# Feed-forward weights loaded and split two chunks at a time, in slabs of eight raw and six split places

## The chip, the cores and the metric

The kernel runs on one core of a Trainium2 chip. The metric is device time in microseconds of one execution, lower is better; the runs before have a median of 2163.3 us.

## The reference

A two-layer encoder on 256 tokens of width 2048, all in float32. Layer 0 mixes tokens by pooling and grouped-query attention, layer 1 by a bidirectional mLSTM. After each mixer comes the same feed-forward layer, which the change is about:

```python
def conv_ffn(x, w_up, conv_w, conv_b, w_down):
    u = x @ w_up                                   # 2048 -> 2 * 5632
    ...
    u = c[0] * up[:, :-2] + c[1] * up[:, 1:-1] + c[2] * up[:, 2:] + conv_b.astype(u.dtype)
    gate, val = jnp.split(u, 2, axis=-1)
    return (jax.nn.silu(gate) * val) @ w_down      # 5632 -> 2048
...
x = x + mixed
x = x + conv_ffn(rms_norm(x, norm_ffn[layer]), w_up[layer], conv_w[layer], conv_b[layer], w_down[layer])
```

## The kernel before

**Weights.** All weights come as one stream of 890 chunks in the order of use, each 128 partitions x 1024 columns (512 KB, rows of 4 KB). `Stream` handles them. `load` starts a DMA on SP's queue into a raw tile w. `split` makes of w a high half, rounded to float32r by a cast on ScalarE (ACT, L152), and a low half, what is left, by a subtraction on VectorE (DVE, L153); both go into a split tile hl. TensorE (PE) multiplies high by high, high by low and low by high. `next` hands out the next chunk's hl and calls `ahead`, which keeps `la` chunks loaded and `sa` chunks split ahead of the one in use. Outside the feed-forward layers there are six raw and four split tiles; inside them one more of each (`more`, L1145), so seven and five, taken in turn.

**The feed-forward layer.** A list from `_ffn_plan` sets TensorE's order by hand. "n" steps are the up-projection (tiles named up, four chunks for 256 of the output columns), "d" steps the down-projection (dn), both of ordinary chunks. "s" steps belong to units (tiles p1 to p6, named by layer, chunk of the hidden width and half: p1_0_21 is layer 0, chunk 2, half 1), which compute four column blocks of the up-projection with seven products instead of eight, out of sums of weight blocks and of activations (sx, made by DVE at the layer's start in `sums`). There are five units a layer; a unit has 28 chunks: 16 for the first half, 12 for the second, where two of three are added in place on DVE before their split (kind "left", L140). Sums of the first half are mostly made ahead by accumulating DMAs from HBM to HBM (tiles G, started by `make_step` when a certain chunk is loaded, on SP and POOL). `UNITS` says between which slots of the list a unit's chunks are strewn. An up or down chunk is 16 or 12 matmuls on TensorE, a unit's chunk 6.

**Who sets the order.** TensorE's order is written by hand; that of ACT, DVE and SP is set by a scheduler when the program is built, and each engine then works its list strictly in order. `Weave` lets small tasks (transposes, convolution tails) run between matmul groups by a planned time.

## Time and profile before

| | |
|---|---|
| runs | 2163.64, 2163.3, 2160.51 us; median 2163.3 |
| profiled execution | span 2160.9 us, granted clock 1.000; no own time beside the span is given, and the fastest run is within 0.4 us of it |
| stages, from the span's start | attention to 256 us, first feed-forward layer to 968, mLSTM to 1448, second feed-forward layer to 2157 |
| SP's loads of 512 KB | about 6 us from issue to landing |
| DMA share of the 16 engines | 0.98 to 0.99 in the first feed-forward layer, 0.74 to 0.91 in the second |

In the rows shown below a group's line reads: source line, engine, operation, output<-inputs by the program's names without numbers, shape and count, then busy time in all and mean nanoseconds of one, then the idle time of that engine just before and what ended it. A timeline row is start, length, engine, line, operation and count, with the idle time before it in brackets. L numbers are lines of this kernel.

### The profile page before, as it was taken

The page shows a single profiled execution, that of the slowest core. Times are in us where ns is not written, and L with a number is a line of the kernel's source. Part 1 is how long each engine was busy: PE and PEld are TensorE (multiplying, and loading weights), DVE is VectorE, ACT ScalarE, POOL GpSimd, SP SyncE. Part 2 cuts the span into 40 slices and gives each one's busy share as a digit, 9 for nine tenths or more (in the row PEclk, how much of TensorE's full clock was granted, in tenths as well). Part 3 has the DMA queues.
Part 4 walks back from the last instruction along what each step waited for, and adds up shares of the span by engine and source line. Part 5 has one row for each costly group of instructions (what it writes and reads, how often), then busy time and mean ns, then how long its engine had stood idle before and what let it go on. Part 6 is the DMA issues. An engine that isn't in the chain of part 4 may idle for free.

```text
span 2160.9 us, 31049 instructions
## 1 busy us (share of the span) xinstructions
PE 2153.2 (100%) x10896; PEld 1826.7 (85%) x10896; DVE 1717.8 (79%) x2400; ACT 1309.2 (61%) x1840; POOL 276.0 (13%) x344
## 2 busy tenths in 40 slices
PE   9999999999999999999999999999999999999999
PEld 7888888888888888888888888888888888888887
DVE  7686698989889797866777677669898888879785
ACT  7665566766557576655454544556676666757663
POOL 0122111111111111111111111110000010000000
PEclk9999999999999999999999999999999999999999
DMA  8878899999999999979998998887999999877773
GB/s 325 257 229 246 256 262 345 316 332 320 308 325 308 351 332 339 319 200 250 250 263 251 256 253 244 258 244 223 312 286 306 302 297 288 272 249 238 259 245 119
DMA packets 204702, 596.15 MB, mean 276 GB/s; under 512 B 26010, under 2 KB 28354, under 8 KB 204546
## 3 DMA queue, kind: packets, MB, share of 16 engines
q1 hardware_dynamic: 167776, 531.43, 70.1%
q0 software_dynamic: 33696, 59.00, 18.3%
q10 hardware_dynamic: 3074, 3.75, 0.9%
q8 instruction: 85, 1.39, 0.2%
q14 instruction: 71, 0.58, 0.1%
HBM read 591.93 MB, written 119.58 MB: 329 GB/s over the span
## 4 chain that ended last, share of the span: by engine, by line
PE 93%; DMA 5%; DVE 1%; ACT 0%; issue 0%; SPq 0%; ACTq 0%; DVEq 0%
PE up L268 23%; PE dn L268 20%; PE p L268 16%; PE op L268 8%; PE mo L268 4%; PE mk L268 4%; PE mq L268 4%; PE mv L268 3%; PE qproj L268 3%; PE kproj L268 1%; PE vproj L268 1%; PE tr L1081 1%; DMA w<-G 1%; PE pool L268 1%; DMA w<-in_m_in 1%; DMA w<-in_up 1%
## 5 line engine op out<-in xcount | busy, mean ns | idle before, releaser
L153 DVE TENSOR_TENSOR hl<-w,hl 128x1024 fp32r<-128x1024 f32 (+2 forms) x892 | 1075.6, 1218 | 319.9 <-ACT hl L152 302.0
L152 ACT CAST hl<-w 128x1024 fp32r<-128x1024 f32 (+2 forms) x891 | 924.8, 1048 | 646.9 <-PE up L268 98.9
L268 PE MATMUL up<-xx,hl 128*128 128x512 f32 (+1 forms) x3072 | 560.2, 337 | 0.0
L268 PEld LDWEIGHTS up<-xx,hl 128*128 128x128 f32 x3072 | 486.7, 188 | 76.7
L268 PE MATMUL dn<-hl,g 128*128 128x512 f32 x2064 | 491.8, 391 | 0.0
L268 PEld LDWEIGHTS dn<-hl,g 128*128 128x128 f32 x2064 | 385.1, 188 | 79.0
L268 PE MATMUL p<-hl,sx 128*128 128x512 f32 x960 | 250.6, 390 | 0.0
L124 POOL DMA_DIRECT2D G<-in_q x160 | 132.0, 830 | 875.5 <-DMA G<-in_q 872.4
L268 PEld LDWEIGHTS p<-hl,sx 128*128 128x128 f32 x960 | 176.0, 188 | 34.4 <-DVE hl L153 0.6
L128 POOL DMA_DIRECT2D G<-G x144 | 127.9, 888 | 538.2 <-DMA G<-in_q 243.0
L268 PE MATMUL p<-hl,xx 128*128 128x512 f32 x720 | 193.5, 390 | 0.0
L268 PEld LDWEIGHTS p<-hl,xx 128*128 128x128 f32 x720 | 130.8, 188 | 24.0
L268 PE MATMUL mk<-xx,hl 128*128 128x512 f32 (+1 forms) x512 | 92.5, 338 | 1.4 <-DVE hl L153 1.4
L268 PE MATMUL mq<-xx,hl 128*128 128x512 f32 (+1 forms) x512 | 92.2, 337 | 0.0
L268 PE MATMUL mv<-hl,xx 128*128 128x512 f32 (+2 forms) x480 | 91.8, 350 | 0.0
L268 PE MATMUL op<-hl,cat 128*128 128x512 f32 x384 | 91.6, 393 | 0.0
L268 PE MATMUL mo<-hl,xx 128*128 128x512 f32 x384 | 90.5, 391 | 0.0
L268 PEld LDWEIGHTS mk<-xx,hl 128*128 128x128 f32 x512 | 79.0, 188 | 13.1 <-DVE hl L153 1.8
L268 PE MATMUL op<-hl,mcat 128*128 128x512 f32 x384 | 89.5, 392 | 0.0
L268 PEld LDWEIGHTS mq<-xx,hl 128*128 128x128 f32 x512 | 79.3, 188 | 11.6
L268 PEld LDWEIGHTS mv<-hl,xx 128*128 128x128 f32 x480 | 78.3, 189 | 11.2
L268 PEld LDWEIGHTS op<-hl,mcat 128*128 128x128 f32 x384 | 71.5, 188 | 14.6
(242 smaller groups left out, 1865.2 us busy)
## 6 DMA issues: line engine op xcount, KB each, us to landing
w<-in_up SPq DMA_DIRECT2D x192, 512.0 KB, 6.1
w<-in_dn SPq DMA_DIRECT2D x176, 512.0 KB, 6.2
w<-in_m_in SPq DMA_DIRECT2D x124, 512.0 KB, 6.0
w<-in_q SPq DMA_DIRECT2D x88, 512.0 KB, 6.2
G<-in_q SPq DMA_DIRECT2D x144, 256.0 KB, 6.4
G<-G POOLq DMA_DIRECT2D x144, 256.0 KB, 7.5
w<-G SPq DMA_DIRECT2D x72, 512.0 KB, 6.1
w<-in_a_in SPq DMA_DIRECT2D x46, 512.0 KB, 6.1
```

Of the source, the lines that this page charges most:

```text
L124: pin(add.dma_start(G[r, 0:512], src[r, 512:1024], accum_op=ALU.add))
L128: pin(add.dma_start(G[:, at : at + 512], G[:, of : of + 512], accum_op=ALU.add))
L152: (self.nc.vector.tensor_copy if i + c == 0 else self.nc.scalar.copy)(hl[:, 0, c : c + n], w[:, c : c + n])
L153: self.nc.vector.tensor_sub(hl[:, 1, c : c + n], w[:, c : c + n], hl[:, 0, c : c + n].bitcast(F32))
L268: pe.matmul(out_, lhsT, rhs, start=start, stop=stop, skip_group_check=True)
L1081: pe.transpose(tr[:, j, t * P : t * P + P], src[:, c : c + P], ident)
```

## The change

In the feed-forward layers chunks are loaded and split in pairs. The raw tiles become places of one slab of six, and of a second slab of two inside these layers; the split tiles places of a slab of four and one of two. A pair takes two neighbouring places. An up or down pair comes with one DMA of 1 MB (rows of 8 KB, the host lays them out so); a unit's chunks still come with DMAs of their own. One cast and one subtraction of 2048 columns split a pair. Three pairs of split places and four of raw ones are in use. The list of steps is counted in pairs, so the units' chunks are strewn in pairs too (`UNITS` halved), and a step of TensorE yields every two chunks. Two sums of kind "left" in one pair become one instruction. Which place is taken is chosen by `Slots.free`; outside these layers chunks stay single.

```diff
+class Slots:
+    def free(self, pair, extra):
+        n = [(100 * b, t.shape[1]) for b, t in enumerate(self.parts) if b == 0 or extra]
+        every = [o + k for o, m in n for k in range(0, m, 2 if pair else 1)]
+        free = [j for j in every if not self.busy.get(j) and not (pair and self.busy.get(j + 1))]
+        return min(free, default=None, key=lambda j: (
+            not pair and not self.busy.get(j ^ 1), max(self.age.get(j, -1), self.age.get(j + pair, -1)), j))
...
 class Stream:
+        self.raw = Slots(wpool.tile([P, 6, CH * P], F32, tag="w", name="w"))
+        self.hls = Slots(spool.tile([P, 4, 2, CH * P], F32R, tag="hl", name="hl"))
...
     def load(self, pieces=1):
-        w = self.home(i, True).tile([P, CH * P], F32, tag="w", name=f"w{i}")
+        pair = self.pair(i)
+        j = self.raw.free(pair, self.extra(i))
+        if j is None:
+            return False
...
+        if pair and got[0][0] == got[1][0] == "half" and got[0][1] is got[1][1] and got[0][2] == 0:
+            sync.dma_start(self.raw.both(j), got[0][1].rearrange("p (a n) -> p a n", a=2))
...
     def split(self, then=None):
+        if pair:
+            w, hl = self.raw.both(self.w[i][0]), self.hls.both(j)
+            self.nc.scalar.copy(hl[:, :, 0], w)
+            self.nc.vector.tensor_sub(hl[:, :, 1], w, hl[:, :, 0].bitcast(F32))
...
     def next(self):
+        if i:
+            self.hls.give(self.hl.pop(i - 1))
...
-                    if q < KT // 4 - 1:
+                    if q == 1:
                         yield
...
-            st.la, st.sa, st.more = 7, 3, (lp(f"fw{layer}", 1), lp(f"fh{layer}", 1), st.at + len(_ffn_plan(layer)))
+            st.raw.parts[1:] = [lp(f"fw{layer}", 1).tile([P, 2, CH * P], F32, tag="w", name=f"fw{layer}")]
+            st.hls.parts[1:] = [lp(f"fh{layer}", 1).tile([P, 2, 2, CH * P], F32R, tag="hl", name=f"fh{layer}")]
+            n = (st.n_load - st.at) % 2
+            st.la, st.sa, st.wide = 9, 4, (st.n_load + n, st.at + 2 * len(_ffn_plan(layer)))
...
-    ((1, 1, 17, 38, 2), (2, 1, 45, 64, 2), (3, 1, 71, 100, 3), (4, 1, 107, 129, 2), (5, 1, 136, 158, 2)),
+    ((1, 1, 8.5, 19, 2), (2, 1, 22.5, 32, 2), (3, 1, 35.5, 50, 3), (4, 1, 53.5, 64.5, 2), (5, 1, 68, 79, 2)),
```

The rows below are lists of the built programs, engine by engine; "x3" are three in a row. In the old program a tile's name has the chunk's number (hl199 is chunk 199's split tile); in the new one w_90 and hl_91 are the slabs of six and four places, fw0 and fh0 those of two, in layer 0.

First place: the second half of layer 0's unit 2 (p1, p5, p6 with 0_21), beside up chunk up0_15. ACT before:

```order
L152 CAST hl193_4776<-w193_4705 128x1024
L152 CAST hl195_4798<-w195_4736 128x1024
L152 CAST hl196_4825<-w196_4752 128x1024
L152 CAST hl199_4869<-w199_4796 128x1024
L152 CAST hl197_4837<-w197_4774 128x1024
L152 CAST hl198_4848<-w198_4785 128x1024
L152 CAST hl200_4880<-w200_4818 128x1024
```

DVE before:

```order
L153 TENSOR_TENSOR hl196_4825<-w196_4752,hl196_4825 128x1024
L140 TENSOR_TENSOR w197_4774<-w197_4774 128x512
L153 TENSOR_TENSOR hl199_4869<-w199_4796,hl199_4869 128x1024
L153 TENSOR_TENSOR hl197_4837<-w197_4774,hl197_4837 128x1024
L153 TENSOR_TENSOR hl198_4848<-w198_4785,hl198_4848 128x1024
L153 TENSOR_TENSOR hl200_4880<-w200_4818,hl200_4880 128x1024
```

Chunk 199 stands ahead of 197 and 198 on both engines. With five places its cast needs chunk 194's, which TensorE must have left. TensorE after, in the same place:

```order
L339 MATMUL up0_15_4242<-xx1_125,fh0_2333 128x512 x2
L339 MATMUL up0_15_4242<-xx1_125,fh0_2333 128x256 x2
L339 MATMUL p5_0_21_3760<-hl_91,sx0_2324 128x512 x3
L339 MATMUL p6_0_21_3772<-hl_91,sx0_2324 128x512 x3
L339 MATMUL p5_0_21_3760<-hl_91,sx0_2324 128x512 x3
L339 MATMUL p6_0_21_3772<-hl_91,sx0_2324 128x512 x3
L339 MATMUL p1_0_21_3759<-hl_91,xx1_125 128x512 x6
L339 MATMUL p5_0_21_3760<-hl_91,sx0_2324 128x512 x3
L339 MATMUL p6_0_21_3772<-hl_91,sx0_2324 128x512 x3
L339 MATMUL up0_15_4242<-xx1_125,fh0_2333 128x512 x2
L339 MATMUL up0_15_4242<-xx1_125,fh0_2333 128x256 x2
```

Call the four pairs k-2 (the up0_15 rows at the top, in fh0), k-1 (p5, p6, p5, p6), k (p1, p5, p6) and k+1 (the next up0_15 rows, in fh0 again). ACT after, with the casts of k-2, k-1, k+1, k and k+2 in this order:

```order
L208 CAST fh0_2333<-fw0_2329 128x2x1024
L1037 CAST g0_2_3568<-y0_14_4113 128x256
L208 CAST hl_91<-w_90 128x2x1024
L208 CAST fh0_2333<-w_90 128x2x1024
L208 CAST hl_91<-w_90 128x2x1024
L208 CAST hl_91<-fw0_2329 128x2x1024
```

DVE after, with the subtractions of k-1, k+1, k and k+2; the adds on w_90 and fw0 are sums for later pairs:

```order
L209 TENSOR_TENSOR hl_91<-w_90,hl_91 128x2x1024
L190 TENSOR_TENSOR w_90<-w_90 128x512
L209 TENSOR_TENSOR fh0_2333<-w_90,fh0_2333 128x2x1024
L190 TENSOR_TENSOR fw0_2329<-fw0_2329 128x512
L209 TENSOR_TENSOR hl_91<-w_90,hl_91 128x2x1024
L209 TENSOR_TENSOR hl_91<-fw0_2329,hl_91 128x2x1024
```

The pair in fh0 that is used last of the four stands ahead of the one in hl_91 that is used before it, on both engines, and its cast overwrites the place of pair k-2.

Second place: SP's queue among the attention weights (in_a_in), from chunk 12 on. Before:

```order
L99 DMA w12_306<-in_a_in 128x1024
L594 DMA x_87<-in_xn 128x2x512
L99 DMA w13_358<-in_a_in 128x1024
L594 DMA x_87<-in_xn 128x2x512
L99 DMA w14_376<-in_a_in 128x1024
L594 DMA x_87<-in_xn 128x2x512
L99 DMA w15_398<-in_a_in 128x1024
L99 DMA w16_419<-in_a_in 128x1024
```

After:

```order
L141 DMA w_90<-in_a_in 128x1024
L665 DMA x_87<-in_xn 128x2x512
L141 DMA w_90<-in_a_in 128x1024
L665 DMA x_87<-in_xn 128x2x512
L124 DMA w_90<-in_up0 128x2048
L166 DMA G021_1_2337<-in_q0 64x512
L168 DMA G021_1_2337<-in_q0 64x1024
L141 DMA w_90<-in_a_in 128x1024 x4
```

A 1 MB load of the feed-forward layer, and a first step for a later unit's sums, now stand among the attention loads: `Slots.free` prefers a place whose neighbour is taken, so from chunk 12 on the attention's chunks go round in four of the six places and the other two are free for it. The mLSTM's chunks go round in four places likewise.

## The prediction

> **What bounds the kernel now.** I read first the page's busy table and its chain, then the busy time by stage, then the TensorE chain for its pace.

> ```profile
> PE 2153.2 (100%) x10896; PEld 1826.7 (85%) x10896; DVE 1717.8 (79%) x2400; ACT 1309.2 (61%) x1840; POOL 276.0 (13%) x344
> PE 93%; DMA 5%; DVE 1%; ACT 0%; issue 0%; SPq 0%; ACTq 0%; DVEq 0%
> ```
> ```profile
> 256.00:610.00 354.00, 354.00 (x1798) 300.42 (x1797) 315.49 (x423) 228.99 (x301) 56.13 (x70) 1.00 0.99 312
> 610.00:968.00 358.00, 357.28 (x1750) 300.60 (x1749) 297.02 (x391) 227.91 (x304) 55.53 (x69) 1.00 0.98 312
> 1448.00:1798.00 350.00, 350.00 (x1776) 297.26 (x1775) 305.56 (x407) 228.01 (x300) 31.65 (x39) 1.00 0.91 285
> 1798.00:2157.00 359.00, 358.60 (x1750) 301.81 (x1748) 289.86 (x376) 216.37 (x278) 7.29 (x9) 1.00 0.74 240
> ```
> ```profile
> 912.76 24.53 PE dn L268 x108
> ```

> The four window rows are the two halves of each feed-forward layer: window, its length, then busy time of PE, PEld, DVE, ACT and POOL, granted clock, DMA share, GB/s. TensorE is idle for 0 + 0.72 + 0 + 0.40 = 1.1 us of 1421 us, at clock 1.00. The last row is a stretch of plain down-projection matmuls: 24.53 / 108 = 227 ns each, 2.73 us for a chunk of twelve. So TensorE is the limit and is nearly never kept waiting; over the whole span it lacks 2160.9 - 2153.2 = 7.7 us. VectorE is busy 315.49 / 354 = 89% in the tightest window: close behind, not the limit.

> How the splits keep up is seen best where they nearly don't. This is the timeline of PE, ACT and DVE at the place that the order above shows (unit p..0_21 beside up0_15):

> ```profile
> 500.75 1.53 PE L268 MATMUL p<-hl,sx 128*128 128x512 f32 x6
> 502.12 1.52 PE L268 MATMUL p<-hl,xx 128*128 128x512 f32 x6
> 503.49 2.94 PE L268 MATMUL up<-xx,hl 128*128 128x512 f32 x16
> 506.26 2.89 PE L268 MATMUL p<-hl,sx 128*128 128x512 f32 x12
> 508.99 2.24 PE L268 MATMUL up<-xx,hl 128*128 128x512 f32 x12
> 503.73 3.90 ACT L152 CAST hl<-w 128x1024 fp32r<-128x1024 f32 x4 [1.84 <-PE p L268]
> 501.92 1.23 DVE L153 TENSOR_TENSOR hl<-w,hl 128x1024 fp32r<-128x1024 f32 x1 [1.25 <-ACT hl L152]
> 503.06 0.69 DVE L140 TENSOR_TENSOR w<-w 128x512 f32<-128x512 f32 x1
> 504.81 4.63 DVE L153 TENSOR_TENSOR hl<-w,hl 128x1024 fp32r<-128x1024 f32 x4 [1.06 <-ACT hl L152]
> ```

> ACT stood still 1.84 us for TensorE: the cast at 503.73 is hl199, whose place is freed when TensorE ends chunk 194 (the p row at 502.12, left at 503.49). Behind it in ACT's and DVE's order stand chunks 197 and 198, which TensorE needs sooner. DVE ends them as the second and third of the four subtractions from 504.81, near 507.2 and 508.3; TensorE reaches 198 at 508.99. Cover: 0.7 us. It holds because between 194 and 198 TensorE still has three chunks (503.49 to 508.99, 5.5 us), against a cast and three subtractions of one chunk each.

> **The change part by part.** First the width. The prices come from these groups:

> ```profile
> L153 DVE TENSOR_TENSOR hl<-w,hl 128x1024 fp32r<-128x1024 f32 x882 | 1067.2, 1222 | 316.4 <-ACT hl L152 298.5 <-DMA G<-in_q 3.7 <-DMA w<-in_m_in 2.4
> L152 ACT CAST hl<-w 128x1024 fp32r<-128x1024 f32 x882 | 918.0, 1051 | 643.9 <-PE up L268 98.9 <-PE dn L268 93.2 <-DVE w L140 90.5
> L966 ACT CAST g<-y 128x256 fp32r<-128x256 f32 x88 | 35.3, 401 | 4.2 <-DVE y L965 4.2
> L986 DVE TENSOR_TENSOR v<-xx 128x2048 f32<-128x2048 f32 x4 | 9.1, 2285 | 0.0
> L140 DVE TENSOR_TENSOR w<-w 128x512 f32<-128x512 f32 x80 | 54.8, 685 | 1.6 <-DMA w<-in_q 1.6
> ```

> DVE has an instruction of 2048 columns already: 2.285 us; two of 1024 take 2.444. For the cast the two ACT rows give (1051 - 401) / 768 = 0.846 ns a column, so 1.051 + 0.867 = 1.92 us against 2.10. Some 156 pairs a layer then save 312 x 0.159 = 50 us of DVE and 312 x 0.184 = 57 us of ACT. Neither engine is on the path, so this buys at most the 1.1 us that TensorE lacks in these layers; I count 0.

> [...]

> Next the depth, which is where I see the price. Five split places of one chunk become three of two. A pair's cast starts when TensorE ends the pair three before it, and the split then takes 1.92 + 2.29 = 4.2 us instead of 2.3; TensorE has two pairs meanwhile. For an up or down pair beside a unit's pair these are 5.5 + 2.73 = 8.2 us (506.26 to 508.99 is a unit's two chunks; 2 x 2.73 a down pair, 2 x 2.77 an up pair from 503.49 to 506.26). The lead falls from 8.2 - 2.3 = 5.9 to 4.0 us. That alone still covers.

> It does not cover where pairs stand out of order. At nine places of the new order (in layer 0 units 0_11 to 0_51, in layer 1 units 1_11, 1_21, 1_31 and 1_51, each in its second half) the casts and the subtractions of pair k stand behind those of pair k+1 on both engines, as the order above shows for 0_21. The cast of k+1 needs the end of pair k-2; after that TensorE has only pair k-1 before it wants k. The chain: 0.24 us from TensorE's next matmul to the cast (503.49 to 503.73); the cast and the hand-over to DVE, 1.92 + 0.03 (503.73 to 504.81 is 1.08 for a 1.05 cast); subtraction of k+1, 2.29, and the sum of another pair that stands between, 0.69, each with the next one starting 0.08 early (501.92 to 503.06 is 1.14 for 1.22); subtraction of k, 2.29. Sum 0.24 + 1.95 + 2.21 + 0.61 + 2.29 = 7.30 us. TensorE's first matmul on k needs only the cast half, so 0.23 comes off: 7.07.
> - Pair k-1 a down pair (0_31, 0_41): 7.07 - 5.46 = 1.6 us each, 3.2.
> - Pair k-1 an up pair (0_51, 1_11, 1_21, 1_51): 7.07 - 5.54 = 1.5 each, 6.1.
> - 0_11 and 1_31, where the sum between is of two chunks (1.22, so 0.53 more): 2.1 and 2.1.
> - 0_21, the place shown: pair k-1 is a unit's pair, 2.73, and the place is freed two matmuls of 0.12 us early ((2.77 - 8 x 0.227) / 8), because the last two of an up chunk read the other half: 7.07 - 2.73 - 0.24 = 4.1.

> Together 17.6 us: 11.0 in layer 0, 6.6 in layer 1. Nothing hides it: TensorE's queue is in order too. Bounds for the unknown width: with two full instructions' time for a pair (2.10 and 2.44) each chain grows by 0.18 + 2 x 0.16 = 0.5 us, 22 us in all; with every hand-over free (0.27 less) and the sums elsewhere (0.6 to 1.1 less) it is 9 us. I take 17.6, since the 2.285 row is the operation itself.

> At each layer's start DVE makes the activation sums (L986 and what follows). From the subtraction of the first unit's first pair to that of the seventh pair behind it, the new order of DVE holds seven subtractions and one add of 2.29 us and 35 instructions of 0.42 to 0.69 us, priced by the rows above and these two:

> ```profile
> L961 DVE SCALAR_TENSOR_TENSOR y<-tb_up,cst,y 128x255 f32<-128x255 f32 x96 | 43.6, 479 | 0.0
> L965 DVE TENSOR_TENSOR y<-y 128x256 f32<-128x256 f32 x88 | 36.8, 420 | 0.9 <-ACT y L964 0.6
> ```

> They sum to 37.3 us, or 33.9 with 0.08 off each of the 43. TensorE has two up pairs, a down pair and four unit pairs meanwhile, 2 x 5.54 + 5.46 + 4 x 2.73 = 27.5 us, and a lead of two up pairs less a split, 11.1 - 4.2 = 6.9. That is 0.5 us short of binding; by full durations it is 2.9 over. I take 1 us for both layers, 0 to 6 as ends.

> The loads and their queue:

> ```profile
> SPq L99 <- DVE hl L153: 1035.9, 563, 6.9
> w<-in_up SPq DMA_DIRECT2D x192, 512.0 KB, 6.1
> w<-in_m_in SPq DMA_DIRECT2D x124, 512.0 KB, 6.0
> ACT hl L152 <- DMA w<-in_m_in: 8.1, 4, 2.4
> ACT hl L152 <- DMA w<-in_dn: 8.1, 8, 2.9
> ```

> SP waits for raw places (1036 us in total), so loads start when a subtraction ends; a landing takes 6 us, and the casts waited little for any. Eight places for seven and a load of 1 MB for two of 512 KB change the feed-forward layers' depth little; the longer landing (512 KB more at 312 GB/s is 1.7 us) eats about what the eighth place gives. Outside these layers raw places now go round in four, not six: a load starts when the chunk four before it is split. Then 6.1 + 2.3 = 8.4 us stand against four chunks, 10.9: hidden. The first 1 MB load of layer 0 is issued on SP already among the attention weights, behind chunk 13: it and its neighbours delay chunk 14 by about 1.4 MB / 312 GB/s = 4.5 us or so, where the lead is several us. I take 1 us for all loads, ends 0 and 15 (a landing that misses by 0.5 us at 30 places). POOL's accumulations keep their order; the PSUM tiles, the end of the kernel and the number of matmuls don't change.

> Sum: 17.6 + 1 + 1 = 19.6 us on the profiled execution's own 2160.9: 2180.5. The runs' median, 2163.3, lies 2.4 above that, so I forecast 2183.

> **The rivals.**
> - Not slower: the reversed pairs don't bind. For it: at the place shown the same reversal left 0.7 us of cover and cost nothing, and DVE has 8% less to do. Against: the chain's links are the engines' own order, and no lead gathered before helps, since the place is freed only by TensorE itself. It decides if the chain of 7.07 us were below 5.5, a third shorter. Then 2163, within 4 us.
> [...]
> - Slower still, by loads in layer 0, where the DMA share is 0.99: if one in four of the 156 pairs lands 0.5 to 1 us late, 20 to 39 us more, 2203 to 2222.
> - Slower still, by the four raw places: if landings in the mixers pass 10.9 - 2.3 = 8.6 us, say by 0.5 us in each of some 50 rounds, 25 us more, near 2208.

> **How the numbers follow.** The forecast, nine reversals that bind and little else, has 72%: its own range is 2170 to 2193 (9 to 22 us for the reversals, 0 to 8 for the rest, and 2 for the runs). Not slower has 9%, faster 3%, layer 0's loads 12%, four places 4%. The range 2168 to 2204 leaves out the first two rivals and most of the last two. A measurement of this kernel can tell about 0.2%, 4.3 us, from no change: faster 3%, same 9%, slower 72 + 12 + 4 = 88%.

> **What would show it.** In the profile of the changed kernel: TensorE idle some 11 us more between 256 and 980 and some 7 us in the second layer, as nine gaps of 1.5 to 4 us that end with DVE's hl, the largest where up0_15 runs; just before each an ACT cast that waited for PE. DVE busy near 1668, ACT near 1252. Stages outside these layers unchanged within 2 us. Wrong would be: gaps spread over many pairs and ended by a DMA (the loads), a longer stage from 970 to 1460 (the four places), or no idle time at TensorE although the casts wait for it.

## The result, and the profile after

The changed kernel takes 2246.5 us (median of 4 runs, 2244.85 to 2248.62) against 2161.9 us before on the same chip: a ratio of 1.0396, 95% interval 1.0383 to 1.0409. The forecast was 2183 us, in a range of 2168 to 2204. The sign was right, and the size a quarter of what came: +20 us against +85.

The page of the changed kernel, busy line and chain:

```profile
PE 2183.4 (97%) x10896; PEld 1839.9 (82%) x10896; DVE 1689.4 (75%) x2062; ACT 1259.8 (56%) x1522; POOL 275.7 (12%) x344
PE 80%; DVE 8%; DMA 6%; ACT 3%; issue 3%; POOL 0%; SPq 0%; ACTq 0%; DVEq 0%; POOLq 0%
```

The span is 2243.0 us, 82.1 more than before. DVE has 28 us less to do and ACT 49 less, and it is TensorE that pays: it stands idle 59.6 us where it stood 7.7, and its same 10896 matmuls are busy 30 us longer. Busy longer for equal work is odd; the clock column of the busy times by stage explains part of it. Columns are window, length, busy time of PE, PEld, DVE, ACT and POOL with counts, granted clock, DMA share, GB/s. The windows begin and end with the same matmuls as those shown of before; the fifth is one of the stretches in which the clock fell.

```profile
261.58:643.93 382.35, 365.48 (x1798) 305.96 (x1797) 310.23 (x339) 216.18 (x221) 57.83 (x72) 0.97 0.95 291
643.93:1019.26 375.33, 362.30 (x1749) 302.79 (x1748) 288.54 (x305) 214.92 (x225) 57.19 (x71) 0.99 0.95 296
1501.84:1872.73 370.89, 357.52 (x1776) 300.43 (x1774) 299.91 (x322) 217.92 (x221) 30.86 (x38) 0.99 0.85 268
1872.73:2238.27 365.54, 360.03 (x1750) 301.57 (x1749) 283.41 (x292) 205.53 (x199) 7.36 (x9) 1.00 0.69 235
337.40:344.20 6.80, 6.38 (x15) 4.64 (x16) 5.23 (x10) 3.09 (x4) 0.95 (x2) 0.50 1.07 339
```

Layer 0 takes 45.6 us more than before (757.7 against 712.1 between the same matmuls), layer 1 28.2 more, attention 5.6 and mLSTM 2.6: 82.0 together. Who keeps TensorE waiting is in its waits (us in total, times, longest), which before had next to nothing in these layers (one wait, of 0.7 us, for c, a sum of a unit's products):

```profile
PE dn L339 <- ACT g L1037: 17.0, 6, 5.9
PE p L339 <- DVE hl L209: 16.5, 9, 2.8
PE p L339 <- ACT tb L1155: 5.0, 4, 2.5
PE up L339 <- DVE xx L405: 4.5, 4, 1.8
PE tr_q L596 <- DVE rot_q L564: 2.9, 2, 2.6
PE dn L339 <- DVE g L1038: 2.9, 2, 2.5
```

The second line is the forecast: nine waits on hl, DVE's subtraction, 16.5 us. The first line was not forecast at all: down-projection matmuls that wait for g, the gated product silu(gate) * val at the end of the convolution's steps. The rest of that family are the sixth line (g's low half, made by DVE) and the third, tb, the units' results on their way into the same convolution. The fourth, xx, are the normalised activations that the up-projection reads.

To see where 82.1 us are, take each matmul's time to the next one's start and subtract the usual pace (227 ns for 512 columns, 116 for 256, 109 for 128, 133 for 288). An excess above 0.25 us counts as a gap and goes to what ended it, or to the gap just before; nine very slow matmuls inside the half-rate stretches, 3.1 us together, are so counted with the gaps. Without them the reversed pairs have 19.1 us, 12.5 in layer 0.

| TensorE's excess over its pace, us | forecast | measured |
|---|---|---|
| gaps before hl, reversed pairs | 17.6 (11.0 + 6.6) | 19.8 (13.2 + 6.6) |
| gaps before g, and before units' matmuls that wait for tb | 0 | 22.6 + 5.7 |
| gaps at the layers' starts (xx) | 1 | 5.4 |
| other gaps (attention, mLSTM, ends), less those of before | 1 (with loads) | 7.2 |
| matmuls at half rate, less those of before | 0 | 17.6 |
| what is left, single matmuls a little late | 0 | 3.8 |
| sum | 19.6 | 82.1 |

**How the wait on g comes about.** ACT, DVE and PE around the longest of them, 5.87 us at 732.24, from the timeline (start, length, engine, line, operation, idle time before it and who ended it):

```profile
712.55 0.56 ACT L1155 COPY tb<-tr 128x512 f32<-128x512 f32 x1
719.62 1.91 ACT L208 CAST fh<-w 128x2048 fp32r<-128x2048 f32 x1 [2.93 <-PE dn L339]
721.43 1.09 ACT L1029 ACTIVATE y<-tb,cst 128x256 f32<-128x256 f32 x2
722.42 1.08 ACT L1029 ACTIVATE y<-tb_up,cst 128x256 f32<-128x256 f32 x2
723.41 3.70 ACT L208 CAST hl<-w 128x2048 fp32r<-128x2048 f32 x2
727.02 0.71 ACT L1035 ACTIVATE y<-y 128x256 f32<-128x256 f32 x2
731.79 0.74 ACT L1037 CAST g<-y 128x256 fp32r<-128x256 f32 x2 [4.05 <-DVE y L1036]
721.56 2.29 DVE L209 TENSOR_TENSOR fh<-w,fh 128x2048 fp32r<-128x2048 f32 x1 [2.03 <-ACT fh L208]
726.53 2.29 DVE L209 TENSOR_TENSOR hl<-w,hl 128x2048 fp32r<-128x2048 f32 x1
729.13 2.28 DVE L209 TENSOR_TENSOR hl<-w,hl 128x2048 fp32r<-128x2048 f32 x1
731.33 0.76 DVE L1036 TENSOR_TENSOR y<-y 128x256 f32<-128x256 f32 x2
732.24 1.65 PE L339 MATMUL dn<-fh,g 128*128 128x512 f32 x3 [5.87 <-ACT g L1037]
```

The convolution's first step (L1029) has its input tb from 713.1 on. It starts at 721.43, because ahead of it in ACT's order stands the cast of a pair into fh, which waits for TensorE to leave that place (719.6). From there the chain to g needs 12.6 us: the cast, four steps, three subtractions of 2.29 us and the steps between them on DVE. The product (L1036) has its input by 727.7, when the last L1035 ends, and starts at 731.33: on DVE too it stands behind a subtraction. TensorE has 6.8 us of work meanwhile, until 726.4. The same place in the kernel before, ACT alone:

```profile
681.77 1.06 ACT L152 CAST hl<-w 128x1024 fp32r<-128x1024 f32 x1 [0.56 <-PE dn L268]
682.73 0.40 ACT L966 CAST g<-y 128x256 fp32r<-128x256 f32 x1
685.89 1.06 ACT L152 CAST hl<-w 128x1024 fp32r<-128x1024 f32 x1 [1.71 <-PE dn L268]
686.85 0.41 ACT L964 ACTIVATE y<-y 128x256 f32<-128x256 f32 x1
688.57 1.06 ACT L152 CAST hl<-w 128x1024 fp32r<-128x1024 f32 x1 [0.30 <-PE p L268]
689.53 0.40 ACT L966 CAST g<-y 128x256 fp32r<-128x256 f32 x1
```

There too casts wait for TensorE with steps of the convolution behind them, but each wait is short, and what follows is one chunk's work. The casts' waits on TensorE over layer 0, before and after:

```profile
ACT hl L152 <- PE up L268: 43.7, 35, 3.1
ACT hl L152 <- PE dn L268: 36.1, 35, 1.7
ACT hl L152 <- PE p L268: 29.9, 51, 3.2
```
```profile
ACT hl L208 <- PE up L339: 39.1, 18, 3.4
ACT hl L208 <- PE dn L339: 34.3, 17, 3.6
ACT fh L208 <- PE up L339: 29.6, 15, 3.5
ACT hl L208 <- PE p L339: 20.5, 15, 5.2
ACT fh L208 <- PE dn L339: 13.0, 6, 6.2
ACT fh L208 <- PE p L339: 10.6, 10, 4.2
```

Before, 109.7 us in 121 waits, 0.91 us each; after, 147.1 us in 81 waits, 1.82 us each. Convolution tails, from the first step to the last, take 11.75 us in the median instead of 9.85, and 20.3 at the longest instead of 14.6.

### The profile page after: what moved, and what is told of

The parts are those of the page before. It is cut to its first block, busy times and chain, and to the rows that moved or that the text cites. A ratio compares the mean times of both kernels' runs of the same rounds, so it can differ in the third digit from the quotient of the medians.

```text
span 2243.0 us, 29520 instructions
## 1 busy us (share of the span) xinstructions
PE 2183.4 (97%) x10896; PEld 1839.9 (82%) x10896; DVE 1689.4 (75%) x2062; ACT 1259.8 (56%) x1522; POOL 275.7 (12%) x344
## 4 chain that ended last, share of the span: by engine, by line
PE 80%; DVE 8%; DMA 6%; ACT 3%; issue 3%; POOL 0%; SPq 0%; ACTq 0%; DVEq 0%; POOLq 0%
PE up L339 20%; PE dn L339 17%; PE p L339 14%; PE op L339 7%; PE mo L339 4%; PE mk L339 3%; PE mq L339 3%; PE mv L339 3%; DVE hl L209 3%; DMA w<-in_up 2%; PE qproj L339 2%; PE pool L339 1%; ACT hl L208 1%; DVE hl L215 1%; DMA w<-in_a_in 1%
## 5 line engine op out<-in xcount | busy, mean ns | idle before, releaser
L209 DVE TENSOR_TENSOR hl<-w,hl 128x2048 fp32r<-128x2048 f32 x158 | 361.7, 2290 | 121.3 <-ACT hl L208 120.5
L215 DVE TENSOR_TENSOR hl<-w,hl 128x1024 fp32r<-128x1024 f32 (+2 forms) x252 | 303.5, 1209 | 172.8 <-ACT hl L213 171.7
L208 ACT CAST hl<-w 128x2048 fp32r<-128x2048 f32 x158 | 301.5, 1910 | 219.8 <-PE up L339 69.0
L213 ACT CAST hl<-w 128x1024 fp32r<-128x1024 f32 (+2 forms) x251 | 260.6, 1041 | 261.1 <-PE op L339 53.7
L339 PE MATMUL up<-xx,hl 128*128 128x512 f32 (+1 forms) x1824 | 332.0, 339 | 0.2 <-DVE hl L215 0.2
L339 PEld LDWEIGHTS up<-xx,hl 128*128 128x128 f32 x1824 | 286.8, 190 | 44.2 <-DVE hl L215 0.7
L339 PE MATMUL up<-xx,fh 128*128 128x512 f32 x1248 | 227.4, 338 | 4.5 <-DVE xx L405 4.5
L209 DVE TENSOR_TENSOR fh<-w,fh 128x2048 fp32r<-128x2048 f32 x80 | 183.2, 2290 | 62.1 <-ACT fh L208 61.7
L339 PEld LDWEIGHTS up<-xx,fh 128*128 128x128 f32 x1248 | 196.2, 189 | 35.7 <-DVE xx L405 5.7
L339 PE MATMUL dn<-fh,g 128*128 128x512 f32 x648 | 160.5, 401 | 20.0 <-ACT g L1037 17.0
L339 PEld LDWEIGHTS dn<-fh,g 128*128 128x128 f32 x648 | 123.7, 193 | 50.1 <-ACT g L1037 19.6
L208 ACT CAST hl<-fw 128x2048 fp32r<-128x2048 f32 x54 | 103.1, 1910 | 72.3 <-issue 17.6
## 6 DMA issues: line engine op xcount, KB each, us to landing
w<-in_m_in SPq DMA_DIRECT2D x124, 512.0 KB, 5.5
w<-in_q SPq DMA_DIRECT2D x64, 512.0 KB, 7.2
w<-G SPq DMA_DIRECT2D x53, 512.0 KB, 6.7
```

What stands on the lines that cost most here:

```text
L208: self.nc.scalar.copy(hl[:, :, 0], w)
L209: self.nc.vector.tensor_sub(hl[:, :, 1], w, hl[:, :, 0].bitcast(F32))
L213: (self.nc.vector.tensor_copy if i + c == 0 else self.nc.scalar.copy)(hl[:, 0, c : c + n], w[:, c : c + n])
L215: self.nc.vector.tensor_sub(hl[:, 1, c : c + n], w[:, c : c + n], hl[:, 0, c : c + n].bitcast(F32))
L339: pe.matmul(out_, lhsT, rhs, start=start, stop=stop, skip_group_check=True)
```

## The experiments

Times are medians; "before" is the kernel before on the same chip, 2160.5 to 2161.0 us in all of these. Diffs are against the changed kernel where nothing else is said.

**e1_order: the reversed pairs alone.** Cast follows cast and subtraction follows subtraction in stream order.

```diff
-            self.nc.scalar.copy(hl[:, :, 0], w)
-            self.nc.vector.tensor_sub(hl[:, :, 1], w, hl[:, :, 0].bitcast(F32))
+            self.behind("cast", self.nc.scalar.copy(hl[:, :, 0], w))
+            self.behind("sub", self.nc.vector.tensor_sub(hl[:, :, 1], w, hl[:, :, 0].bitcast(F32)))
...
+    def behind(self, what, ins):
+        last = self.made.get(what)
+        if last is not None:
+            self.tc.add_manual_dep(ins.ins, last, mybir.DependencyInfo(
+                mybir.DependencyClass.NoSync, mybir.DependencyReason.DATA), reason="split_order")
+        self.made[what] = ins.ins.name
```

> The changed kernel with one edit: the casts of the pairs are held in stream order on ACT, and the subtractions on DVE, so the nine reversed places are gone; width, places and loads stay. Theory R (reversed pairs, as forecast): the ten gaps of TensorE that DVE's or ACT's hl ends in the feed-forward layers (19.1 us by start-to-start excess) and the half-rate matmuls right behind three of them (1.5 + 2.0 + 1.2 us) go, the waits on the convolution chain stay: 2246.5 - 24 = 2222 us. Rival P (the pairs are late everywhere, the reversals only show it first): the same waits turn up at other pairs, 2240 to 2250 us.

Measured: 2225.1 us, ratio to before 1.0293 (1.0278 to 1.0308), so 21.4 less than the changed kernel. TensorE's waits:

```profile
PE dn L346 <- ACT g L1044: 16.2, 6, 5.9
PE p L346 <- ACT tb L1162: 5.5, 4, 2.5
PE p L346 <- DVE hl L216: 4.0, 6, 1.4
```

The waits on hl fall from 16.5 to 4.0 us, those on g and tb stay. Theory R is shown, as one quarter of the loss.

**e4_512 and e3_loads: the loads alone.** e4_512 loads each pair with two DMAs of 512 KB; e3_loads keeps the 1 MB loads, but splits chunk by chunk into six places (it also makes the sums of kind "left" one by one, and takes outside places in turn, as in e8_plain below).

```diff
 e4_512
-        if pair and got[0][0] == got[1][0] == "half" and got[0][1] is got[1][1] and got[0][2] == 0:
+        if False and got[0][0] == got[1][0] == "half" and got[0][1] is got[1][1] and got[0][2] == 0:
 e3_loads, in split
-        pair = self.w[i][5]
+        pair = False
```

> The changed kernel with one edit: a pair of up or down chunks is loaded by two DMAs of 512 KB in place of one of 1 MB; casts and subtractions of 2048 columns, places and order stay. Theory L (the large loads land late): 2200 us or less. Theories R, D and W: the loads aren't the cause, 2242 to 2251 us.

> The loads of the changed kernel without its splits: 1 MB loads into pairs of raw places, but each chunk has its own cast and subtraction of 1024 columns and its own split place of six, in whatever order the program gives, and places outside these layers go round in six. Theory D: no waits on g or on hl in the feed-forward layers, 2158 to 2172 us. Theory L (the loads have a price that the pairs hide): 2180 us or more.

Measured: e4_512 2250.6 us (1.0413, 1.0397 to 1.0428), as slow as the changed kernel; e3_loads 2164.9 us (1.0016, 1.0007 to 1.0026), four us above before, with no wait on g or hl. A 1 MB landing takes longer, 6.1 us before for 512 KB of in_up against, in the changed kernel,

```profile
w<-in_up SPq DMA_DIRECT2D x65, 1024.0 KB, 7.4
```

and costs at most those four us. The loads are not the cause of the other 80. A load of 1 MB neither helps nor harms here by more than some 4 us: 2246.5 us with it and 2250.6 without in the paired kernel, 2164.9 with it and 2160.5 without where chunks are split singly.

**e9_nord and e2_rev: two instructions for a pair.** Both hold the order as e1_order does.

```diff
 e9_nord
+            for k in range(2):
+                self.behind("cast", self.nc.scalar.copy(hl[:, k, 0], w[:, k]))
+                self.behind("sub", self.nc.vector.tensor_sub(hl[:, k, 1], w[:, k], hl[:, k, 0].bitcast(F32)))
 e2_rev
+            for k in (1, 0):
+                self.behind("cast", self.nc.scalar.copy(hl[:, k, 0], w[:, k]))
+            for k in (0, 1):
+                self.behind("sub", self.nc.vector.tensor_sub(hl[:, k, 1], w[:, k], hl[:, k, 0].bitcast(F32)))
```

> As the run with the order held, and each pair split by two casts and two subtractions of 1024 columns, the second half's cast first. So both casts still stand until TensorE has left the whole pair three before (release by pairs), but no instruction is wider than 1024. Theory W (width: one cast of 1.91 and one subtraction of 2.29 us keep ACT and DVE from the short steps of the convolution): the waits for g and for the transposed sums (22.6 and 5.7 us of gap, some 9 us of half-rate matmuls behind them) mostly go, 2185 to 2195 us. Theory D (release by pairs: a waiting cast at the head of ACT's queue, and the subtraction behind it on DVE, hold up the short steps): they stay, and the splits take some 0.4 us longer a pair: 2220 to 2240 us.

> As the run before, but the first half's cast and subtraction come first, each half waiting for its own chunk alone (release by chunks, six places); order held, 1 MB loads, pairs of places unchanged. Theory D: the waits for g and for splits go, only the mixers' 9 us stay: 2165 to 2175 us. Theory W: no further gain over the run with two instructions a pair in which the halves are released together, both near 2190 us. Theory L (1 MB loads are the cause): 2220 us or more, as with the order held.

Measured: e2_rev 2232.0 us (1.0332, 1.0317 to 1.0347), e9_nord 2181.9 us (1.0103, 1.0087 to 1.0120; its runs spread from 2174.8 to 2186.3). The waits on g stay in e2_rev:

```profile
PE dn L348 <- ACT g L1046: 19.7, 6, 6.2
```

In the profiled execution of e9_nord, its fastest, the waits on g, tb and hl of these layers no longer appear. It looked like theory D, that a cast must wait for a whole pair, though e9_nord is 7 us above the range that D gave it.

**e12_touch and e12b_touch_end: the release alone.** e9_nord, and ahead of a pair's casts ACT makes a small copy into the pair's second half, so that the casts stand until TensorE has left that half.

```diff
 e12_touch
+            self.behind("cast", self.nc.scalar.copy(hl[:, 1, 0, 0:64], w[:, 1, 0:64]))
 e12b_touch_end
+            self.behind("cast", self.nc.scalar.copy(
+                hl[:, 1, :, 0:1024:64], w[:, 1, 0:1024:32].rearrange("p (a n) -> p a n", a=2)))
```

> As e9_nord (order held, two casts and two subtractions of 1024 columns a pair, first half first), and ahead of each pair's casts ACT copies 64 columns into the pair's second half, which is cast again right after. So the casts again wait until TensorE has left both chunks of the pair three before, though the first half is ready some 1.6 us sooner than in e1_order. Theory D (what waits at the head of ACT's queue holds up the convolution chain): near e1_order and e2_rev, 2210 to 2235 us, with waits on g of 15 us or more. Rival Q (only the lateness of the first half counts): near e9_nord, 2175 to 2195 us.

> As e12_touch, but the small copy ahead of each pair's casts now writes 32 columns spread over the whole second half, high and low part, so that it waits for TensorE's last matmul on the pair (in e12_touch it was released before that). Then two casts and two subtractions of 1024 columns, first half first, order held. Theory G (what counts is that the first cast waits for the whole pair three before): 2205 to 2235 us, near e1_order. Theory Q (what counts is how late the first half is ready after its release, 2.5 us here and 4.2 us in e1_order): 2180 to 2195 us.

Measured: 2186.2 us (1.0122, 1.0108 to 1.0136) and 2183.9 us (1.0110, 1.0095 to 1.0125). In e12_touch the copy was released before the half was left for good: the casts behind it still wait 66 us for TensorE. In e12b_touch_end all the waiting, 227 us, is the copy's, and the casts behind it wait for TensorE no more. Yet it is within e9_nord's own spread, and no wait on g is left. So theories D and G fall: with half-wide instructions, releasing by pairs is not what costs.

**b4: a smaller lead in the kernel before.** Diff against the kernel before.

```diff
-                (self.spool if i % 5 < 4 else self.more[1]))
+                self.spool)
```

> The kernel before with one edit: its feed-forward layers split into four places in turn, not five; chunks stay single, loads and widths as before. A cast then starts when TensorE ends the chunk four before it, three chunks ahead of use: 1.37 + 1.37 + 2.77 = 5.5 us against a split of 2.3, so a lead of 3.2 us, below the 4.0 us of the paired kernel. Theory D with the lead as its measure: waits on g and on splits as in the paired kernel, 2190 to 2230 us. Rival C (what counts is that two chunks are taken and given back together, not the lead): 2160 to 2172 us.

Measured: 2166.6 us (1.0029, 1.0019 to 1.0040). With 3.2 us of lead, less than the paired kernel's 4.0, chunk-wise splits cost 6 us. Rival C has the number; against its reason speaks e12b_touch_end, where ACT too waits for both chunks of a pair. A lead counted in us, my measure in the prediction, does not tell the two apart.

**e15_cast_narrow and e16_sub_narrow: one engine at a time.** e1_order with the cast, or the subtraction, in two halves.

```diff
 e15_cast_narrow
+            for k in range(2):
+                self.behind("cast", self.nc.scalar.copy(hl[:, k, 0], w[:, k]))
 e16_sub_narrow
+            for k in range(2):
+                self.behind("sub", self.nc.vector.tensor_sub(hl[:, k, 1], w[:, k], hl[:, k, 0].bitcast(F32)))
```

> e1_order with two casts of 1024 columns a pair, each waiting for its own chunk, and still one subtraction of 2048. Theory G: the first cast no longer stands until the whole pair is left, ACT's queue moves on a chunk earlier, 2180 to 2200 us. Theory Q: the first half is ready no sooner than in e1_order, since the one subtraction needs both casts: 2215 to 2235 us.

> e1_order with one cast of 2048 columns a pair, which waits for the whole pair, and two subtractions of 1024. Theory G: 2210 to 2235 us. Theory Q: the first half is ready 1.1 us sooner than in e1_order, part of the way, 2200 to 2215 us. Theory W (the 2.29 us instruction on DVE is what the short steps wait for): 2180 to 2195 us.

Measured: 2209.6 us (1.0222, 1.0206 to 1.0237) and 2229.9 us (1.0324, 1.0307 to 1.0340). Against e1_order that is 15.5 less and 4.8 more, while both halves together, in e9_nord, give 43.2 less. Theory G has the second and misses the first by 10 us; Q, which e12b_touch_end had borne out, misses both, and so does W. In e15_cast_narrow the waits on g drop to 3.3 us, and the transposes behind the units wait for DVE instead:

```profile
PE tr L1161 <- DVE c L1136: 11.2, 8, 2.9
PE up L347 <- DVE xx L413: 7.6, 3, 3.1
PE dn L347 <- ACT g L1045: 3.3, 3, 1.4
```

That is a first sign that the wait moves rather than goes.

**e19_opin, e20_opinplain, e21_nopinplain: order by force.** Each pair's cast and subtraction also go behind whatever the program wrote before them.

```diff
 e19_opin (e20: the same with e8_plain's edit; e21: e20 with e9_nord's two halves)
         self.made[what] = ins.ins.name
+        self.tc.keep_in_program_order(ins)
```

> e1_order with one edit: each pair's cast and subtraction also stand behind whatever the program wrote before them on the same engine, so the convolution's steps go ahead of casts that wait for TensorE. Casts and subtractions stay 2048 wide, places are released by pairs, loads are 1 MB. Theory O (the order alone): the waits on g and on the transposed sums and the half-rate stretches behind them go, 2170 to 2192 us, the mixers' waits stay. Theory W (width): 2215 us or more. A new price is possible under O: a split that now stands behind a convolution step which is not ready comes late, seen as waits on hl.

> e19_opin, and outside the feed-forward layers the place given back longest ago is taken (as in e10_nordplain). Theory O: some 12 us below e19_opin, 2158 to 2178 us, since e10 was 15.6 us below e9; with the width free of price it comes near e10's 2166 us.

> e20_opinplain with two casts and two subtractions of 1024 columns a pair, first half first. If the width has no price once the order is right: within 6 us of e20_opinplain. If it has one: e20 is 10 us or more above this one, which would then be 2158 to 2168 us.

Measured: 2404.1 us (1.1122), 2387.5 us (1.1049) and 2265.6 us (1.0482). A clear miss, by the new price that the expectation named: splits now stand behind steps that aren't ready, and TensorE waits for splits everywhere (e19_opin):

```profile
PE p L347 <- DVE hl L217: 27.8, 20, 1.8
PE dn L347 <- ACT hl L216: 21.3, 8, 4.9
PE dn L347 <- DVE fh L217: 17.0, 9, 2.9
```

They show how much the order on ACT and DVE can cost. They also answer what e21 was for: under the same rule of order, full width costs 122 us more than half width (2387.5 against 2265.6; the half-wide casts also wait for their own chunk alone).

**x1_order_of_e12b: e12b's places for the convolution's steps, at full width.** Every convolution step, from L1029 of the changed kernel on, is held between the same two pairs as in e12b_touch_end, on ACT ("a") and DVE ("v"); numbers are how many pairs stand ahead of it. What makes their input tb_up out of an up-projection's result, a copy on ACT and two steps on DVE, is not held.

```diff
+PLACES = {
+    (0, 0): {'a': [3, 3, 4, 5], 'v': [3, 3, 3, 3, 4, 5]},
...
+    def step(self, ins, at):
+        done = self.pairs.setdefault(ins.ins.engine, [])
+        if 0 < at <= len(done):
+            self.after(ins, done[at - 1].ins.name)
+        if at < len(done):
+            self.after(done[at], ins.ins.name)
+        else:
+            self.steps.append((at, ins.ins.engine, ins.ins.name))
```

> e1_order at full width, with each convolution step of the feed-forward layers held, on ACT and on DVE, between the same two pairs as in e12b_touch_end (a table of 88 rows); two casts and two subtractions there, one of each here. Theory O (only the order matters): the waits on g go and nothing else comes, 2180 to 2195 us. Theory W' (with one cast and one subtraction a pair either the short steps or the splits are late, and the order only chooses which): the waits on g go, and waits on hl and on DVE's sums behind the units (tr) of about the same sum take their place, 2210 to 2235 us.

Measured: 2218.2 us (1.0272, 1.0245 to 1.0299), 7 less than e1_order and 34 more than the kernel whose order it takes. Its waits, in an execution of 2227.1 us:

```profile
PE p L456 <- DVE hl L326: 13.0, 16, 1.8
PE tr L1275 <- DVE c L1250: 6.0, 5, 2.2
PE dn L456 <- DVE fh L326: 2.6, 3, 1.8
PE up L456 <- DVE fh L326: 2.0, 4, 1.0
PE dn L456 <- DVE g L1160: 1.5, 2, 1.0
PE p L456 <- DVE fh L326: 1.2, 4, 0.6
```

The 19.4 us of waiting on g in e1_order (16.2, and 3.2 on DVE's half of g) are 1.8 here (1.5, and 0.3 on ACT's half); the 4.0 on hl are 18.8 on hl and fh (13.0 + 2.6 + 2.0 + 1.2), and tr has grown from 2.0 to 6.0. That fits theory W': at full width either the short steps or the splits are late, and the order only chooses which. Shown is that the waits on g come from where the steps stand, since only the order was changed. That full width must pay one way or the other is not shown, because this is not quite e12b_touch_end's order. The copies tb_up stand a pair later in 36 of 48 cases, and ACT waits 82.1 us, 34 times, at the head of its queue for a tb_up that a held step needs (in e12b_touch_end the held steps wait 0.6 us for it, and it is the copy that waits, 94.9 us, for TensorE's up). Right behind such a step stands the late cast of three of the waits on splits (at 756, 789 and 2012 us, 3.2 us together).

The traces of the runs above say the same of the waits on g. How far back g's cast stands in ACT's list, counted in casts of 1024 columns (a full-wide cast is two) and against its place in e9_nord, mean of 88:

| kernel | g's cast stands later by | TensorE's waits on g, us |
|---|---|---|
| e2_rev, half-wide | 1.35 | 23.2 |
| e1_order, full-wide | 1.33 | 19.4 |
| e16_sub_narrow | 1.33 | 20.4 |
| e15_cast_narrow | 0.56 | 4.2 |
| e12_touch, half-wide | -0.03 | 0.9 |
| e12b_touch_end, half-wide | -0.61 | 0 |
| x1_order_of_e12b, full-wide | -0.67 | 1.8 |

The waits go with the place and not with the width: the half-wide e2_rev has them, the full-wide x1_order_of_e12b has hardly any. The edits of e2_rev, e9_nord, e15, e16 and the two e12 runs name only the splits; the place of g's cast moved because the scheduler made another list.

**e8_plain, e10_nordplain, e18_ahead3: what lies outside.** A place is taken by age alone.

```diff
-            not pair and not self.busy.get(j ^ 1), max(self.age.get(j, -1), self.age.get(j + pair, -1)), j))
+            max(self.age.get(j, -1), self.age.get(j + pair, -1)), j))
 e10_nordplain: e9_nord with it; e18_ahead3: e3_loads with
-            st.la, st.sa, st.wide = 9, 4, (st.n_load + n, st.at + 2 * len(_ffn_plan(layer)))
+            st.la, st.sa, st.wide = 8, 3, (st.n_load + n, st.at + 2 * len(_ffn_plan(layer)))
```

> The changed kernel with one edit: outside the feed-forward layers a load or split takes the place given back longest ago, with no preference for one whose neighbour is taken. Theory M (four raw places in turn there cost the mixers and the layers' ends time): the stages outside gain what e10 gained on e9, 8 to 16 us, 2230 to 2238 us. Otherwise 2243 to 2250 us.

> As e9_nord, and single chunks outside the feed-forward layers take the place that was given back longest ago, with no preference for one whose neighbour is taken, so raw places go round in six again. Theory M (the four raw places delay attention and mLSTM): TensorE's gaps at attention's queries (66 us) and at mLSTM's first products (1005 to 1009 us), 2.6 and 2.0 us, and those that follow go: 2170 us or less in median, 6 us or more below e9_nord. Otherwise: 2175 to 2185 us.

> e3_loads with splits running three chunks ahead of use as in the kernel before, and loads eight, not four and nine. If the 4 us that e3_loads is above the kernel before come from splits that stand ahead of the activation sums on DVE at the layers' starts (2.5 us of waiting on xx), 2158 to 2163 us; if from the larger loads, 2164 to 2167 us.

Measured: e8_plain 2237.7 us (1.0352, 1.0335 to 1.0369), 8.8 less than the changed kernel; e10_nordplain 2166.2 us (1.0028, 1.0018 to 1.0038), 15.6 less than e9_nord; e18_ahead3 2168.7 us (1.0037, 1.0025 to 1.0050). In e8_plain attention's wait at 66 us (2.9 on rot_q) is gone and that stage ends at 255.8 us, as before, not at 261.6; mLSTM takes 4.3 us less. So the four raw places cost some 9 us. The last 4 to 6 us over before, in e3_loads and e10_nordplain, lie in the feed-forward layers. In e3_loads they are four gaps of the first one, 0.9, 0.9 and 1.8 us at its start, where DVE makes the activations, and 2.1 us at 779 us for c. Why DVE is late there stays open: e18_ahead3, with fewer splits ahead, missed both of its ranges; it keeps gaps of 0.9 and 1.8 us there and has 3.5 us of new ones before g. None of these kernels beats the one before.

## Why the prediction was wrong

- **Reversed pairs** (17.6 us): right, 19.8 measured, 6.6 for 6.6 in layer 1. The largest is at 0_21 as forecast, 0.88 and 2.83 us of waiting at 523.8 and 527.1. Taken in order of time, seven of the nine come within 0.1 us of their own sums; the first (2.5 for 2.1) and the fourth (2.65 for 1.6) don't. The chain of a cast and two subtractions was read from the right rows; e1_order takes it away for 21.4 us.
- **Depth**: here the prediction failed. "The lead falls from 8.2 - 2.3 = 5.9 to 4.0 us. That alone still covers" asks only whether TensorE's next split is in time. A cast that waits for TensorE also stands ahead of the convolution's steps in ACT's order, and its subtraction ahead of them on DVE, and TensorE needs their result within a few pairs. I named what stands behind the waiting cast at the nine reversals, casts and subtractions, and gave every other consumer of these two queues nothing; the row of ACT's g and y stood in my own fence as a price for the cast's width. The result is 28.3 us of gaps. The runs show that neither the release by pairs (e12b_touch_end) nor the lead (b4) makes them. They come from how far behind the splits the scheduler puts the convolution's steps: x1_order_of_e12b moves the steps alone, and the waits on g fall from 19.4 to 1.8 us at full width. With half-wide instructions, first half first, there is an order in which steps and splits are both in time; in none of the orders run at full width (the changed kernel's, e1_order's, the program's, x1_order_of_e12b's) are they.
- **Half-rate matmuls**, 17.6 us: left out. Every gap was priced at its length.
- **Width**: no gain for TensorE, as said. The saving itself was over-estimated on DVE, 28 us for 50: two instructions back to back overlap by 0.08 us in the busy time (before, four subtractions from 504.81 take 4.63 us, not 4 x 1.222 = 4.89), so each of 318 pairs (312 in the prediction) saves 2 x 1.222 - 2.290 - 0.08 = 0.07 us, 24 in all. On ACT it was 49 us for 57. One way of breaking instructions up let TensorE finish sooner: e9_nord is 43 us below e1_order with 25 us more to do on DVE. Breaking up alone is not enough: e16_sub_narrow and e2_rev do it too and are 4.8 and 6.9 us above e1_order.
- **Layers' starts**: 5.4 us for 1, inside the ends of 0 and 6.
- **Loads and raw places**: loads right (e3_loads, e4_512). "Hidden" for the four places was wrong by some 9 us, at attention's queries and in mLSTM; the rival of 25 us there did not come.
- **Of the rivals**, layer 0's loads did not show: no DMA is among what TensorE waits for. The chance of 3% for a faster kernel has no support in any run: loads of 1 MB landed in 7.4 us where 512 KB took 6.1, and without them e4_512 took 2250.6 us for 2246.5.

Open: how the 43 us between e1_order and e9_nord divide among the cast, the subtraction and the order that the scheduler makes of them (15.5 less, 4.8 more and 7 less when changed singly); what full width costs in an order made for it, since no run holds all of e9_nord's or e12b_touch_end's order at full width; and the 4 to 6 us that stay without any pairing of splits.

## What to carry to other kernels

Before two instructions are merged on an engine that works its list in order, as ACT did here (until 719.62 it stood still 2.93 us at a cast that waited for TensorE, with L1029's input ready since 713.1 behind it), list everything that stands behind them there, not only their own consumer: a wait at the head of the queue is passed on to the short steps behind it, and their deadline may be tighter than yours (12.6 us of chain against 6.8 us of TensorE's work above). Here merging made each wait twice as long (0.91 to 1.82 us), and what follows it too, and the 28 us of busy time saved on DVE and 49 on ACT, neither of them the limit, bought nothing for that: the span grew by 82.1. Where a scheduler makes the order, read its new list for those short steps before you blame width or depth. When an engine without slack gets gaps, look at its granted clock beside them: here 17.6 us of half-rate matmuls came on top of the gaps.

## What the hardware showed

The eleven stretches cost 1.0 to 2.2 us each, 17.6 together, so by these figures a wait of 3 us that brings one on costs an estimated third to three quarters more than its length.
